# Cross-attention output projections in a two-layer encoder: seven block products inside one plan per layer

## The chip, the cores and the metric

The kernel runs on one core of one Trainium2 chip. The metric is the device time of one execution in microseconds (us), the median of the runs. Engines are named as in the profile: PE is TensorE's matrix multiply, DVE is VectorE, ACT is ScalarE, POOL is GpSimd, and SP is SyncE, whose queue issues the transfers between memory and the chip. R, X, XV, scr are buffers in SBUF; pA and pB are PSUM tiles.

## The reference, cut to what matters

The program is a two-layer encoder over 1024 tokens with 1024 channels, all in float32. Layer 0 mixes tokens by grouped-query attention, layer 1 by a pooling mixer. Both then cross-attend into 256 memory tokens and pass a gated MLP.

```
for i in range(DEPTH):                       # DEPTH = 2
    if i % N_MIXERS == 0:
        x = x + axial_gqa_attention(rmsnorm(x, attn_norm[ia]), ...)
    else:
        x = x + multiscale_pool_mixer(rmsnorm(x, pool_norm[ib]), ...)
    x = x + memory_cross_attention(rmsnorm(x, xattn_norm[i]), rmsnorm(mem, mem_norm[i]), ...)
    x = x + conv_gated_ffn(rmsnorm(x, ffn_norm[i]), ...)
return rmsnorm(x, final_norm)

def memory_cross_attention(h, mem_n, w_q, w_kv, w_o):
    q = (h @ w_q).reshape(b, s, X_HEADS, X_HEAD_DIM) * (X_HEAD_DIM ** -0.5)
    ...
    scores = jnp.einsum('bshd,bmhd->bhsm', q, k).astype(jnp.float32)
    p = jax.nn.softmax(scores, axis=-1).astype(v.dtype)
    o = jnp.einsum('bhsm,bmhd->bshd', p, v).reshape(b, s, D_MODEL)
    return o @ w_o
```

The change concerns the last line, `o @ w_o`, a product of 1024 x 1024 by 1024 x 1024 in each layer, and how the work around it is ordered.

## The kernel before

**Numbers in two halves.** PE multiplies a rounded format (fp32r), so each operand is kept as a high part, made by ACT (`high`, L667), and the rest, the low part, made by DVE as source minus high (`low`, L670). A product of two operands is three matmuls, high by high, high by low and low by high (`mm3`, L752 to L757), each of 128 rows by 512 columns. ACT comes before DVE for every operand, and both before PE.

**Slots.** High and low parts lie in 20 tiles of 2048 columns, handed out in halves (`Slots`, L88): 40 halves in all. Six scratch tiles `scr` hold what transfers bring in. Eight row tiles X0 to X7 (two of them called XV) hold the residual stream, 128 tokens each; they also serve as scratch while the stream is stored in memory (`Xq`, `Xd`).

**The plan.** `Plan` (L161) is a list scheduler that runs while the program is built. Every operation is added with its engine, a cost, what it reads and writes, the slots and PSUM banks that it takes, and perhaps a due time. PE's operations keep the order in which they are added, and PE's clock gives their due times; all others get the latest time at which their readers still come in time, and are emitted in the order in which the simulated engines could take them, at most 30 us (`AHEAD`) before they are due. The result is a fixed order for each engine and for SP's queue.

**Seven products.** `Seven` (L299) multiplies a 2 x 2 block matrix by another in seven block products instead of eight (the Strassen-Winograd form): sums S1 to S4 of the left blocks, T1 to T4 of the right ones, and results that are added up in PSUM and read between products. The query projection, the MLP's up-projection and the down-projection use it. `plan_turned` (L478) transposes a normalised row tile on PE and makes its blocks; `plan_late` (L512) makes T2 to T4; `plan_first` and `plan_early` (L580, L601) load and sum the first weights.

**The output projections.** `rows_by` (L1852) gives a block of one row tile by 512 columns: eight k-steps of `mm3`, 24 matmuls, then a DVE addition (L1864) to the row. It is called for 8 row tiles x 2 column halves. `Seven.begin` (L448) runs these 16 blocks in an order written by hand (`steps`, `turns`, `extras`, `loads`): a block, perhaps the transposes of a row tile that is done, the addition, the store of that half row (`save`, L313), and after the second half of a row the squared sum on ACT, the root on POOL and the scaling on DVE (`norm`, L317). It serves three places: layer 0's attention projection ahead of the query projection (`load_rows`, L706, loads its second column half at the start), and both layers' cross-attention projections ahead of the up-projection. Layer 1's query projection follows the pooling mixer (`pool_mixer`, L2334), which is part of a plan; it stores whole rows (L2447) before it scales them (L319).

**The cross-attention.** `cross` (L1527) plans the query products, keys and values, scores, transposes of the probabilities (`plan_turn`, L1696), and the values (`plan_values`, L1720): 16 products of 6 matmuls, whose results ACT and DVE turn into high and low parts. The weights w_o come in eight loads of 512 KB, each with one `high` and one `low` of 1024 columns (`plan_weights`). One plan ends there; the hand-written part follows; then the MLP's plan (`ffn_main`, L1899) begins. `down_sums` (L1814) loads blocks of the down-projection's weights, forms T1 to T4 on DVE and stores them in memory (`Wt`), some while the query products run; `plan_W` (L2028) loads blocks and sums back and splits them.

```
steps = ((0, 0), (0, 2), (1, 0), (1, 2), (0, 4), (1, 4), (0, 6), (1, 6),
         (0, 1), (1, 1), (0, 3), (1, 3), (0, 5), (0, 7), (1, 5), (1, 7))
turns = {3: 0, 4: 2, 6: 4, 8: 6, 10: 1, 12: 3, 15: 5}
```

Each pair is (column half, row tile); `turns` gives after which step which row tile is transposed.

Of the kernel before, what the change touches and what calls it, by code (L numbers as in the profile page):

```python
# [10 lines left out]
F32 = mybir.dt.float32  # L11
# [149 lines left out]
class Plan:  # L161
# [12 lines left out]
    def __init__(self, slots, free, room):  # L174
        self.slots = slots
        self.free = {"PE": 0.0, "DVE": 0.0, "ACT": 0.0, "POOL": 0.0, "SP": 0.0, **free}
        self.room = {pool: [0.0] * n for pool, n in room.items()}
        self.ops, self.last, self.since, self.users, self.clock = [], {}, {}, {}, 0.0
        self.known, self.pools, self.ended = {}, {}, {}

    def add(self, kind, n, emit, reads=(), writes=(), take=(), uses=(), gives=None, late=None, room=None):
# [4 lines left out]
        elif room:  # L186
# [5 lines left out]
              "begin": 0.0, "due": float("inf"), "after": [], "keys": [k for _, k in take if k] + list(uses)}  # L192
# [36 lines left out]
    def run(self):  # L229
        pools = self.pools  # L230
# [13 lines left out]
        def begin(op):  # L244
# [54 lines left out]
class Seven:  # L299
# [6 lines left out]
    def __init__(self, kn, w, columns, X, Xd, gain):  # L306
# [3 lines left out]
        self.began = False  # L310


    def save(self, n, t):  # L313
        c = slice(n * 512, (n + 1) * 512)
        self.nc.sync.dma_start(out=self.Xd[t * P:(t + 1) * P, c], in_=self.X[t][:, c])

# [4 lines left out]
    def turn(self, t):  # L321
        self.ps[t] = [self.kn.psB() for _ in range(2)]
# [4 lines left out]
    def parts(self, name, t):  # L327
        if name not in self.H:
            self.H[name] = [self.R.get(), self.R.get()]
        return (self.R.v(s, 4)[:, :, t // 2 * P:(t // 2 + 1) * P] for s in self.H[name])  # L330

    def keep(self, name, t, src):
        self.kn.hi_lo(*self.parts(name, t), src.rearrange("p (a b) -> p a b", a=4))

    def late(self, name, t):

        lo, hi = self.LO, self.HI
        src = {"T2": self.X[t][:, hi], "T3": self.X[t][:, lo], "T4": self.X[t - 1][:, hi]}[name]
        self.keep(name, t, src)
# [3 lines left out]

    def take1(self, t):
        nc, ps, lo, hi = self.nc, self.ps[t], self.LO, self.HI
        x, y = self.X[t - t % 2], self.X[t]
        nc.scalar.copy(y[:, lo], ps[0])
        if t % 2:
            self.sub(nc.vector, x[:, lo], ps[0], x[:, lo])
            self.sub(nc.vector, y[:, hi], ps[1], x[:, lo])  # L350
            self.sub(nc.vector, y[:, lo], ps[1], y[:, lo])

    def take2(self, t):
        nc, ps, lo, hi = self.nc, self.ps.pop(t), self.LO, self.HI
        x, y = self.X[t - t % 2], self.X[t]
        if t % 2 == 0:
            nc.scalar.copy(y[:, hi], ps[1])
            self.keep("B11", t, ps[0])
            self.keep("B21", t, ps[1])
        else:  # L360
            self.keep("T1", t, x[:, lo])
            self.keep("B22", t, ps[1])
            if t < 4:
                self.fourth(nc.gpsimd, t)

    def fourth(self, e, t):
        x, y, hi = self.X[t - 1], self.X[t], self.HI
        self.sub(e, x[:, hi], x[:, hi], y[:, hi])

# [6 lines left out]

    def first_load(self, f, n):

        self.raws[f] = [self.kn.scr() for _ in range(n)]
        self.place[f] = [f"raw{f}{j}" for j in range(3)]  # L380
        for j in range(min(n, 2)):
            self.load(f, j)
# [23 lines left out]
    def split(self, f, *names):  # L406
        for name in names:
            self.high(f, name)
            self.low(f, name)


# [4 lines left out]
    def product(self, f, n):  # L416
# [9 lines left out]
        bh, bl = (R.v(s, 4) for s in self.H[right])  # L426
        for k in range(4):
            self.kn.mm3(u[bank], ah[:, k], al[:, k], bh[:, k], bl[:, k], not more and k == 0, k == 3, more)
# [19 lines left out]
    def begin(self, gemm, add, free, between):  # L448

        late, split, self.began = self.late, self.split, True  # L450
        steps = ((0, 0), (0, 2), (1, 0), (1, 2), (0, 4), (1, 4), (0, 6), (1, 6),
                 (0, 1), (1, 1), (0, 3), (1, 3), (0, 5), (0, 7), (1, 5), (1, 7))
        turns = {3: 0, 4: 2, 6: 4, 8: 6, 10: 1, 12: 3, 15: 5}
        extras = {5: between,
                  13: lambda: [self.sum(0, n) for n in ("S1", "S2", "S3")],
                  14: lambda: (split(0, "A12", "A11"), late("T2", 1), late("T2", 3)),
                  15: lambda: late("T3", 1)}
        loads = {10: lambda: self.first_load(0, 3), 12: lambda: self.first_load(1, 1)}
        for i, (n, t) in enumerate(steps):
            gemm(n, t)  # L460
            free(n, t)
            u = turns.get(i)
            if u is not None:
                self.turn(u)
            extras.get(i, lambda: None)()
            add(n, t)
            self.save(n, t)
            loads.get(i, lambda: None)()
            if n:
                self.r[t] = self.kn.row_rstd(self.X[t])  # L470
            if u is not None:
                self.take1(u)
            if n:
                self.norm(t)
            if u is not None:
                self.take2(u)

    def plan_turned(self, plan, t):  # L478
# [6 lines left out]
        banks = [("turned", t, g) for g in range(2)]  # L485
# [3 lines left out]
        plan.add("turn", 8, lambda: self.turn(t), [X(t, 0), X(t, 1)], banks, [("B", k) for k in banks])  # L489
# [12 lines left out]
    def plan_keep(self, plan, name, t, src, *keys, uses=(), late=None):  # L502
        parts = lambda: self.parts(name, t)
        shaped = lambda: src().rearrange("p (a b) -> p a b", a=4)
        plan.add("copy", 512, lambda: self.kn.high(list(parts())[0], shaped()), keys, [("H", name, t)],
                 (), uses, late=late, room=None if name in self.H else (("H", name), 4))
        plan.add("add", 512, lambda: self.kn.low(*parts(), shaped()), [*keys, ("H", name, t)], [("H", name, t)], uses=uses, late=late)
# [4 lines left out]
    def plan_late(self, plan, second, third, fourth):  # L512
# [4 lines left out]
        for t in second:  # L517
            self.plan_keep(plan, "T2", t, at(self.X[t], hi), X(t, 1))
        for t in third:
            self.plan_keep(plan, "T3", t, at(self.X[t], lo), X(t, 0))  # L520
        for t in fourth:
# [5 lines left out]
    def plan_rest(self, plan):  # L527

        if self.began:
            plan.known.update({(f"X{NT - 1}", h): 5.4 for h in range(2)})  # L530
        self.plan_turned(plan, NT - 1)
        self.plan_late(plan, *((5, 7), (3, 5, 7), (5, 7)) if self.began else [(1, 3, 5, 7)] * 3)
# [1988 lines left out]
```

## Time and profile before

| | us |
|---|---|
| median of 3 runs | 2390.1 |
| lowest and highest run | 2388.69, 2391.19 |
| the profiled execution's own time | 2389.2 |
| its span, first to last instruction | 2387.5 |

The profile comes from one execution. A row of a group of instructions names its line, engine and operation, output and inputs, shapes and count, then the busy time in us and the mean of one in ns, then the engine's idle time just before and what ended it. A timeline row gives the start in us, the duration, engine, line, operation; in square brackets stands how long the engine was idle before it and for whom it waited. A window row gives, for a stretch of time, the busy time of each engine with its count of instructions. The durations of matmuls overlap, so their spacing is read from their starts.

### The profile page before, as it was taken

How to read it: one execution, taken by the hardware profiler on the slowest of the kernel's cores; microseconds unless marked ns; L12 is line 12 of the kernel's file. 1: busy time of each engine (PE TensorE's matmuls, PEld its weight loads, DVE VectorE, ACT ScalarE, POOL GpSimd, SP SyncE). 2: the span in 40 equal slices, each digit the busy share in tenths (PEclk: the TensorE clock that was granted, in tenths of full speed). 3: DMA queues.
4: the chain of work that ended last, by engine and by line, in shares of the span. 5: the costliest groups of instructions: out<-in, count | busy, mean ns of one | idle time of the engine just before them, and what ended most of it. 6: DMA issues, size and time to landing. Idle time of an engine off the chain costs nothing.

```text
span 2387.5 us, 32617 instructions
## 1 busy us (share of the span) xinstructions
PE 2373.0 (99%) x11855; PEld 1899.5 (80%) x11855; DVE 1863.1 (78%) x2608; ACT 1201.0 (50%) x1983; POOL 407.0 (17%) x393
## 2 busy tenths in 40 slices
PE   9999999999999999999999999999999999999998
PEld 8764444788988888888888888898888888888887
DVE  6679998569863898888887768986389888888875
ACT  6555556335552655455454427555255555545542
POOL 5577777210110000000000013011000000000001
PEclk9999999999999999999999999999999999999999
DMA  7000002426851243334477633695124333447852
GB/s 257 1 1 15 20 15 55 155 76 228 315 173 63 71 133 89 111 89 121 134 260 245 201 92 121 231 323 198 62 71 132 89 110 89 118 134 247 277 190 102
DMA packets 323436, 322.93 MB, mean 135 GB/s; under 512 B 32612, under 2 KB 253132, under 8 KB 323276
## 3 DMA queue, kind: packets, MB, share of 16 engines
q1 hardware_dynamic: 323132, 320.85, 41.7%
q8 instruction: 93, 1.52, 0.3%
q14 instruction: 67, 0.55, 0.1%
q10 hardware_dynamic: 144, 0.00, 0.0%
HBM read 233.30 MB, written 82.64 MB: 132 GB/s over the span
## 4 chain that ended last, share of the span: by engine, by line
PE 78%; DVE 2%; ACT 0%; DMA 0%; issue 0%; POOLq 0%; POOL 0%; DVEq 0%
PE pB L755 22%; PE pB L756 22%; PE pB L757 22%; PE pA L757 3%; PE pA L755 3%; PE pA L756 3%; PE pB L324 1%; DVE R L671 1%; PE pA L2392 0%; PE pB L1703 0%; PE pA L1703 0%; DVE X L319 0%; DMA scr<-in_ffn_w_down 0%; DVE X L342 0%; DMA Xq<-X 0%
## 5 line engine op out<-in xcount | busy, mean ns | idle before, releaser
L756 PE MATMUL pB<-R,R 128*128 128x512 f32 (+1 forms) x2735 | 1030.9, 377 | 2.6 <-DVE R L677 1.6
L755 PE MATMUL pB<-R,R 128*128 128x512 f32 (+1 forms) x2671 | 1010.6, 378 | 0.9 <-DVE R L671 0.8
L757 PE MATMUL pB<-R,R 128*128 128x512 f32 (+1 forms) x2673 | 1006.1, 376 | 0.0
L756 PEld LDWEIGHTS pB<-R,R 128*128 128x128 f32 x2735 | 515.1, 188 | 97.1 <-DVE R L677 2.6
L755 PEld LDWEIGHTS pB<-R,R 128*128 128x128 f32 x2671 | 503.0, 188 | 96.2 <-DVE R L671 1.3
L757 PEld LDWEIGHTS pB<-R,R 128*128 128x128 f32 x2673 | 503.2, 188 | 92.0 <-DVE R L671 0.5
L668 ACT ACTIVATE R<-scr 128x512 fp32r<-128x512 f32 (+3 forms) x370 | 264.5, 745 | 225.1 <-DMA scr<-Gs 55.8
L671 DVE TENSOR_TENSOR R<-scr,R 128x512 fp32r<-128x512 f32 (+2 forms) x334 | 282.1, 874 | 26.2 <-ACT R L668 22.1
L728 POOL TENSOR_SCALAR ms<-ss 128x1 f32<-128x1 f32 x52 | 12.6, 242 | 1628.8 <-ACT R L2374 629.1
L671 DVE TENSOR_TENSOR R<-X,R 128x512 fp32r<-128x512 f32 (+1 forms) x262 | 178.1, 688 | 49.3 <-ACT R L668 48.8
L668 ACT ACTIVATE R<-X 128x512 fp32r<-128x512 f32 (+1 forms) x262 | 163.8, 632 | 86.9 <-PE pB L756 53.2
L438 ACT COPY scr<-pB 128x512 f32<-128x512 f32 x156 | 91.4, 586 | 197.9 <-PE pB L757 191.2
L807 DVE TENSOR_REDUCE nm<-pS 128x1 f32<-128x512 f32 x232 | 148.2, 682 | 20.0 <-PE pS L801 18.6
L1326 ACT ACTIVATE X<-pT 128x1024 f32<-128x1024 f32 x128 | 125.1, 1023 | 72.2 <-PE pT L1319 69.6
L757 PE MATMUL pA<-R,R 128*128 128x512 f32 (+1 forms) x420 | 150.2, 358 | 0.0
L755 PE MATMUL pA<-R,R 128*128 128x512 f32 (+1 forms) x416 | 149.0, 358 | 0.0
L756 PE MATMUL pA<-R,R 128*128 128x512 f32 (+1 forms) x416 | 148.4, 357 | 0.0
L1361 PE MATMUL pO<-X,XV 128*64 128x512 f32 x512 | 124.1, 605 | 0.0
L2080 DVE TENSOR_TENSOR X<-pB,X 128x512 f32<-128x512 f32 (+1 forms) x110 | 75.2, 684 | 62.2 <-PE pB L757 61.7
L440 DVE TENSOR_TENSOR scr<-pB,scr 128x512 f32<-128x512 f32 x156 | 106.7, 684 | 11.7 <-PE pB L757 11.6
L1319 PE MATMUL pT<-R,R 64*128 64x512 f32 x768 | 103.2, 393 | 0.4 <-DVE R L671 0.4
L668 ACT ACTIVATE R<-pB 128x256 fp32r<-128x256 f32 (+1 forms) x139 | 62.6, 483 | 80.2 <-PE pB L757 43.5
(252 smaller groups left out, 2890.9 us busy)
## 6 DMA issues: line engine op xcount, KB each, us to landing
Gs<-X SPq DMA_DIRECT2D x105, 256.0 KB
X<-in_ffn_w_up SPq DMA_DIRECT2D x51, 512.0 KB
scr<-in_ffn_w_down SPq DMA_DIRECT2D x43, 512.0 KB
scr<-Gs SPq DMA_DIRECT2D x35, 512.0 KB
scr<-in_xattn_w_kv SPq DMA_DIRECT2D x32, 512.0 KB
XV<-in_ffn_w_up SPq DMA_DIRECT2D x31, 512.0 KB
scr<-Gs SPq DMA_DIRECT2D x40, 384.0 KB
Wt<-scr SPq DMA_DIRECT2D x44, 256.0 KB
```

The source lines that it names most:

```text
L438: self.nc.scalar.copy(out, p)
L440: self.nc.vector.tensor_tensor(out=out, in0=p, in1=out, op=OP.add)
L668: self.nc.scalar.activation(hi, src, AF.Copy)
L671: self.nc.vector.tensor_tensor(out=lo, in0=src, in1=hi.bitcast(F32), op=OP.subtract)
L755: mm(out, ah, bh, start=start, stop=False)
L756: mm(out, ah, bl, start=False, stop=False)
L757: mm(out, al, bh, start=False, stop=stop)
L807: nc.vector.tensor_reduce(NM[G][:, 2 * n + x.start:2 * n + x.stop], S, axis=AX.X, op=OP.max, negate=True)
L1319: nc.tensor.matmul(T[G, kt % 2][:, x * 512:(x + 1) * 512], left, right, start=first and (i, j) == (0, 0), stop=shifted or (not first and i ...
L1326: nc.scalar.activation(E[G, kt], T[G, kt % 2], AF.Exp)
L1361: nc.tensor.matmul(O[G][x * HD:(x + 1) * HD], V32[kt // 4][:, kt % 4, m // 4 * 2 + x], E[G, kt][:, x * 512:(x + 1) * 512], start=kt == 0, ...
L2080: nc.vector.tensor_tensor(out=x, in0=banks[k][:, c], in1=x, op=OP.add)
```

## The change

Both hand-written orders go (`begin`, `rows_by`, `load_rows`), and each layer becomes a single plan from its mixer's or attention's projection to the down-projection.

- **The cross-attention's projection as seven products.** The left matrix is the attention output; its blocks come straight from the value products: A11 and A12 from the even row tiles, A22 and the sums S1 to S4 as the odd ones arrive (`plan_values`). The columns of two of the four row tile pairs (group 0) are split at once; of the S sums those of group 1 are parked in memory as float32 (`Lt`) and loaded and split later (`plan_parked`, the items "L"). The right blocks and sums T1 to T4 of w_o are formed by DVE ahead of time and stored (`weight_sums`, the items "S" of ATT and the steps in OUT_AT), then loaded and split (`weight_blocks`, the items "W"). `plan_product` adds each product to its row.
- **The attention's projection** of layer 0 keeps its 16 blocks of 24 matmuls, now as planned operations in the order ATT (`attention_out`).
- **Stores.** Every row is stored in two halves as each is ready (`plan_save`), the pooling mixer's too; the squared sum goes to a slot instead of PSUM (`plan_norm`).
- **Due times.** With `follow`, the plan moves the due times of the other engines' operations by the largest delay that PE has had so far in the simulation.
- Tiles may lie in two separate halves (`get_pair`, `parts`); some transposes go to pA (`wide`); the table of the convolution is planned (`conv_table`).

```diff
+OUT = [("P", 1), ("P", 3), ("X", 0), ("G",), ("W", 0), ("V", 0, 1), ("X", 2), ("P", 5), ("V", 0, 3), ("V", 0, 0),
+       ("V", 0, 2), ("P", 7), ("V", 0, 5), ("V", 0, 7), ("V", 0, 4), ("V", 0, 6), ("X", 4), ("X", 6), ("O", 2, 0, 0),
+       ("V", 1, 0), ("V", 1, 1), ("O", 2, 0, 1), ("V", 1, 2), ("V", 1, 3), ("W", 1), ("O", 2, 1, 0), ("V", 1, 4),
+       ("V", 1, 5), ("W", 2), ("O", 2, 1, 1), ("V", 1, 6), ("O", 1, 0, 0), ("W", 3), ("X", 1), ("V", 1, 7), ("X", 3),
+       ("O", 1, 0, 1), ("O", 5, 0, 0), ("O", 5, 0, 1), ("O", 6, 0, 0), ("O", 6, 0, 1), ("O", 3, 0, 0), ("X", 5), ("X", 7),
+       ("O", 7, 0, 0), ("O", 3, 0, 1), ("O", 7, 0, 1), ("L", "S1"), ("T", 0), ("O", 4, 0, 0), ("O", 4, 0, 1), ("L", "S2"),
+       ("L", "S4"), ("L", "S3"), ("E",), ("O", 1, 1, 0), ("C",), ("O", 1, 1, 1), ("O", 5, 1, 0), ("T", 2), ("O", 5, 1, 1),
+       ("O", 6, 1, 0), ("T", 1), ("O", 6, 1, 1), ("O", 3, 1, 0), ("O", 3, 1, 1), ("T", 3), ("O", 7, 1, 0), ("O", 7, 1, 1),
+       ("T", 4), ("O", 4, 1, 0), ("T", 6), ("O", 4, 1, 1)]
+OUT_AT = (30, 42, 54, 66)
+UP = [(2, 0), 5, (1, 0), (2, 1), None]
+QUERY = [(2, 0), 5, (1, 0), (2, 1), None], [3, (2, 0), 5, (1, 0), (2, 1), None]
+ATT = [("X", 1), ("W",), ("X", 3), ("D", 0, 0), ("D", 0, 2), ("D", 0, 1), ("S",), ("D", 0, 4), ("D", 0, 3), ("D", 1, 0),
+       ("S",), ("D", 0, 6), ("D", 1, 2), ("X", 5), ("T", 0), ("S",), ("D", 1, 4), ("T", 2), ("S",), ("X", 7), ("D", 1, 6),
+       ("T", 4), ("D", 1, 1), ("D", 1, 3), ("E",), ("T", 6), ("D", 0, 5), ("T", 1), ("D", 1, 5), ("D", 0, 7), ("T", 3),
+       ("D", 1, 7)]
...
-            return t if op["engine"] == "PE" else max(t, op["due"] - self.AHEAD)
+            return t if op["engine"] == "PE" else max(t, op["due"] + drift - self.AHEAD)
...
-                    if u < t + op["busy"] and other["due"] < min(t + op["busy"], op["due"]):
+                    if u < t + op["busy"] and other["due"] < min(t + op["busy"] - drift, op["due"]):
...
+            if e == "PE" and self.follow:
+                drift = max(drift, t - op["at"])
...
+    def plan_save(self, plan, t, h):
+
+        def save():
+            c = slice(h * 512, (h + 1) * 512)
+            self.nc.sync.dma_start(out=self.Xd[t * P:(t + 1) * P, c], in_=self.X[t][:, c])
+        plan.add("load", 0.5, save, [(f"X{t}", h)], [("saved", self.tag, t, h)], late=1.0)
...
+            if not par:
+                plan_cut(plan, ("A11", "A12")[o], n, lambda: sm[b], [b], [b], 5.0)
+                plan.add("copy", 512, keep, [b], x[o:o + 1], uses=[b], late=4.0)
+                return
+            if not o:
+                plan.add("add", 512, third, [b, x[0]], s[:1], [("scr", s[0])], [b, s[0]], late=2.0)
+                return
+            plan.add("add", 512, second, [b, s[0]], s[1:], uses=[b, s[0]], late=3.0)
+            plan_cut(plan, "A22", n, lambda: sm[b], [b], [b], 5.0)
+            plan.add("add", 512, first, [s[1], x[0]], x[:1], uses=s[:1], late=5.0)
+            plan.add("add", 512, fourth, [s[1], x[1]], x[1:], uses=s[:1], late=6.0)
+            for name, t, h, k in (("S1", A, 0, x[0]), ("S2", SX, 1, s[1]), ("S4", A, 1, x[1]), ("S3", SX, 0, s[0])):
...
+                plan_cut(plan, name, n, lambda t=t, at=at: t[n][:, at:at + 256], [k], uses, 9.0 if uses else None)
+                plan.add("load", 0.25, park, [k], [("Lt", name, n)], uses=uses, late=9.0 if uses else 10.0)
...
+        def plan_product(plan, n, g, j):
+
+            left, right, bank, name, h = U.PRODUCTS[n]
+            p = 2 * g + j
+            b, t, fresh, ws = ("xo", bank, p), 2 * p + (name == "v"), n in (2, 1, 5), [("xw", k, right) for k in range(4)]
...
+                for k in range(4):
+                    self.mm3(outs[b], *(R.hv(z)[:, k * 256 + j * P:k * 256 + (j + 1) * P] for z in hs),
+                             *(R.hv(WD[k, right])[:, c] for c in (slice(0, 512), slice(512, 1024))),
+                             fresh and k == 0, k == 3, not fresh)
...
+            plan.add("product", 12, emit, ins + ws, [b], [("A" if bank == "x" else "B", b)] if fresh else (), ws + ([] if fresh else [b]),
+                     ("half", 2) if j else None)
+            plan.add("add", 512, read, [b, (f"X{t}", h)], [(f"X{t}", h)], uses=[b], late=1.5)
+            if n not in (2, 5, 6):
+                F.plan_save(plan, t, h)
+            if n in (3, 4):
+                F.plan_norm(plan, t, "fgain")
...
-            for par in range(2):
-                for m in range(NK):
-                    if not par and m % 2 == 0:
-                        plan_turn(plan, m + 1)
-                    plan_values(plan, par, m)
...
+    def attention_out(self, OT, plan, U, X):
...
+            plan.add("product", 24, gemm, [("rows", t // 4)] + [("wrow", g, k) for g in range(2) for k in range(2) if n], [b], [("B", b)],
+                     gives=("half", 8 * end + 4 * out) if end or out else None)
+            plan.add("add", 512, add, [b, *x], x, uses=[b])
+            U.plan_save(plan, t, n)
             if n:
-                free(t)
+                U.plan_norm(plan, t, "gain")
```

In OUT, "P" transposes probabilities, "V" is a value product (parity, index), "X" loads a row tile back, "W" loads and splits a group of weight blocks, "O" is a block product (product, group, tile within the group), "L" loads parked sums, "T" transposes a finished row tile, "E" starts the up-projection's first weights. In ATT, "D" is a block (column half, row tile) and "S" a round of weight sums.

More of the change, by code (lines that the diff above doesn't have):

```diff
@@ L1738, in plan_values, with keep, third @@
-            plan.add("copy", 512, lambda: self.high(list(place())[0], sm[b]), [b], [key], (), [b], late=3.0, room=(("O", par, m // 2), 2))
-            plan.add("add", 512, lambda: self.low(*place(), sm.pop(b)), [b, key], [key], uses=[b], late=3.0)
+                if last:
+                    R.put_half(*(h for z in PT.pop(par) for h in z), *(v if par else ()))
+            def keep():
+                A[n] = X[spots[n]]
+                nc.scalar.copy(A[n][:, mine], sm[b])
+            def third():
+                SX[n] = self.scr()
+                nc.vector.tensor_tensor(out=SX[n][:, :512], in0=A[n][:, :512], in1=sm[b], op=OP.subtract)
@@ L1741, in main @@
         def main():
             order, parts = U.order(nf), [(c, m) for c in range(8) for m in range(2)]
[L1743 to L1750 removed]
+            plan = Plan(R, over, {"scr": 6, "A": 2, "B": 4, "half": len(R.freed)}, True)
```

577 lines of the change are left out of this document (296 added, 281 removed).

## The prediction

> **What bounds the kernel now.** I read the page first: engine shares, busy tenths, then the chain that ended last.
>
> ```profile
> span 2387.5 us, 32617 instructions
> PE 2373.0 (99%) x11855; PEld 1899.5 (80%) x11855; DVE 1863.1 (78%) x2608; ACT 1201.0 (50%) x1983; POOL 407.0 (17%) x393
> ...
> PEclk9999999999999999999999999999999999999999
> ...
> PE 78%; DVE 2%; ACT 0%; DMA 0%; issue 0%; POOLq 0%; POOL 0%; DVEq 0%
> ```
>
> TensorE (PE) is busy 99% of the span at full clock, and the chain runs through it. So a stage is worth what its matmuls take, unless something else comes to end last there. A busy time of overlapping matmuls isn't the price of one; the timeline of a stretch without waits gives that:
>
> ```profile
> 447.42 0.39 PE L755 MATMUL pB<-R,R 128*128 128x512 f32 x1
> ...
> 452.64 0.39 PE L757 MATMUL pB<-R,R 128*128 128x512 f32 x1
> ```
>
> These are the first and last of 24 matmuls: 23 steps in 5.22 us, 0.227 us each. Next, the windows of the stages that the change touches; columns are busy time with count of PE, weight load, VectorE (DVE), ScalarE (ACT), POOL, then clock, DMA share, GB/s.
>
> ```profile
> 442.60:531.80 89.20, 87.60 (x417) 72.31 (x416) 44.60 (x57) 29.69 (x55) 10.45 (x21) 1.00 0.28 96
> 531.80:608.00 76.20, 76.20 (x363) 63.99 (x362) 72.13 (x105) 44.35 (x71) 2.44 (x4) 1.00 0.68 232
> 676.40:706.50 30.10, 30.10 (x150) 25.07 (x148) 24.88 (x36) 23.28 (x42) 1.85 (x4) 1.00 0.52 177
> 706.50:803.50 97.00, 97.00 (x462) 80.51 (x461) 45.53 (x61) 28.54 (x53) 8.54 (x18) 1.00 0.19 66
> 1190.00:1420.00 230.00, 229.90 (x1013) 189.74 (x1012) 175.36 (x243) 98.26 (x136) 2.88 (x3) 1.00 0.61 203
> 1443.00:1495.00 52.00, 49.14 (x348) 44.52 (x348) 46.62 (x69) 36.32 (x69) 12.28 (x21) 1.00 0.26 97
> ```
>
> In order: layer 0's attention projection; its query products; the cross-attention's values; its output projection; layer 0's down-projection; layer 1's pooling mixer. Only the mixer and the first leave PE idle. In the second DVE is busy 72.13 of 76.2 us (95%) and PE loses nothing: a nearly full DVE needn't cost PE anything.
>
> **The change part by part.**
>
> 1. *Fewer products.* Before, a layer's output projection is 16 blocks of 8 x 3 matmuls, 384. After: 7 products x 2 groups x 2 row tiles x 4 x 3 = 336. Two layers save 96, at 0.227 us 21.8 us. The transposes (8 per row tile, and the table's 4) and the attention projection's 384 matmuls keep their number. All of it is on the path.
>
> 2. *The attention projection inside the plan.* The waits of PE show what goes:
>
> ```profile
> 442.50 0.40 PE L755 MATMUL pB<-R,R 128*128 128x512 f32 x1
> 443.78 0.50 PE L756 MATMUL pB<-R,R 128*128 128x512 f32 x1 [0.88 <-DVE R L677]
> ...
> 445.04 0.39 PE L755 MATMUL pB<-R,R 128*128 128x512 f32 x1
> 446.15 0.50 PE L756 MATMUL pB<-R,R 128*128 128x512 f32 x1 [0.72 <-DVE R L677]
> ```
>
> The third block, the first of the right columns, waits for its weights' low parts. Its steps are 1.28 and 1.11 us instead of 0.227: 1.9 us lost. After, right columns come sixth, three blocks (16.3 us) later, while the last low part ends near 446.1: -1.9 us. What comes earlier is row tile 1's block, third instead of ninth; its input row is the first load, and only its addition needs it. New in this stage are four rounds of weight sums (2 loads of 512 KB, 4 subtractions, 4 stores of 256 KB each): 16 subtractions at 0.7 us, 11 us of DVE on 44.60 of 89.2, and 8 MB at a DMA share of 0.28. Layer 1's rounds fall into 1190 to 1420: 175 + 11 of 230 us. Hidden, 0; without that cover each late round costs PE some 0.7 us per subtraction.
>
> 3. *DVE in the new output stage.* This decides whether the 21.8 us arrive. The prices, from the groups of instructions by form (the first two and the fourth within the stages above):
>
> ```profile
> L671 DVE TENSOR_TENSOR R<-pB,R 128x512 fp32r<-128x512 f32 x20 | 13.5, 686 | 3.5 <-ACT R L668 3.5
> L671 DVE TENSOR_TENSOR R<-scr,R 128x1024 fp32r<-128x1024 f32 x7 | 8.4, 1220 | 0.5 <-ACT R L668 0.5
> L671 DVE TENSOR_TENSOR R<-scr,R 128x512 fp32r<-128x512 f32 x201 | 131.2, 685 | 11.3 <-ACT R L668 7.2 <-PE pB L757 4.1
> L1864 DVE TENSOR_TENSOR X<-pB,X 128x512 f32<-128x512 f32 x12 | 8.3, 690 | 21.2 <-PE pB L757 21.2
> L671 DVE TENSOR_TENSOR R<-pB,R 128x256 fp32r<-128x256 f32 x70 | 27.6, 418 | 25.5 <-ACT R L668 20.2 <-PE pB L801 5.2
> L1828 DVE TENSOR_TENSOR X<-X,X 128x512 f32<-128x512 f32 x20 | 13.8, 690 | 0.6
> L668 ACT ACTIVATE R<-X 128x512 fp32r<-128x512 f32 x260 | 162.2, 630 | 86.9 <-PE pB L756 53.2 <-DVE X L394 23.4 <-DMA X<-in_ffn_w_up 5.1
> L668 ACT ACTIVATE R<-pB 128x256 fp32r<-128x256 f32 x76 | 26.6, 385 | 56.4 <-PE pB L757 31.1 <-PE pB L1162 25.3
> L668 ACT ACTIVATE R<-scr 128x1024 fp32r<-128x1024 f32 x97 | 101.1, 1059 | 77.4 <-PE pB L756 32.0 <-DMA scr<-Gs 14.5 <-DMA scr<-in_xattn_w_kv 9.6
> ```
>
> Removed per layer: 16 value lows x 0.686, 8 weight lows x 1.220, 16 additions x 0.690 = 31.8 us. Added: 12 lows of A11, A12, A22 x 0.686 = 8.2; 16 sums (third, second, first, fourth) x 0.690 = 11.0; 16 half-width lows x 0.418 = 6.7; 4 parked lows x 1.220 = 4.9; 28 weight lows x 0.685 = 19.2; 28 additions x 0.690 = 19.3; together 69.3. The stage now takes 30.1 + 97.0 = 127.1 us with DVE 70.4 busy; after, PE needs 127.1 - 10.9 = 116.2 and DVE 70.4 - 31.8 + 69.3 = 107.9, or 93%. That is full, but under the 95% at which the query products lose nothing. ACT gets 28 + 12 + 8 copies of at most 0.630, 16 of 0.385 and 4 of 1.059 (40.6 us), and sheds 16 of the first and 8 of the last kind (18.6), on 23.28 + 28.54: 73.8 us, 64% of 116.
>
> The tight place: after the last value product, one output product (2.7 us) hides second sum, first sum, ACT's high and the low of S1: 0.69 + 0.69 + 0.385 + 0.418 = 2.2 us plus hand-overs. Likewise at the up-projection's start, where the last row tiles need addition, square, root and scaling. So some short waits. From both sides: 0, as in 531.8 to 608; or the mixer's rate, 2.86 of 52 us at 90% DVE, over 116 us 6.4 per layer. The query stage is the nearer row (the same seven products, planned alike), but the hand-overs are tighter: 1.5 us per layer, **+3.0**.
>
> 4. *DMA of the stage.* Removed: 8 loads of 512 KB. Added: 7 MB of weight blocks, 16 parks of 128 KB, 4 reloads of 512 KB; net 7 MB over 116 us, 60 GB/s on 66 to 177, where 232 GB/s already ran beside a full PE. SP issues some 32 more, hidden under loads planned up to 30 us ahead; the cost without that cover is the second rival below.
>
> 5. *Rows in halves; due times that move.* Layer 1's mixer has them. The chain of waits and the timeline there:
>
> ```profile
> 1444.70 4.57 DMA Xq<-X
> ...
> 1451.95 1.25 PE L324 MATMUL pB<-ident,X 128*128 128x128 f32 x8 [0.71 <-ACT XV L488]
> ```
>
> Scaling a row overwrites what the store reads, so it waits 4.57 us for a 512 KB store; two halves let the first go one block earlier and the last one be shorter. I take the 0.7 us that PE waits behind it: **-0.7**. The later waits (1463 to 1493) lie where DVE has no gap and stay. Moving due times by the delay changes only in which order ready work is taken; no row shows it. Bounds of the term: -2.9 (the mixer's whole loss goes) and +2 (an order that is worse by as much again).
>
> The Trainium skill ("DMA: Bandwidth & Descriptors", Anatomy of one DMA) gives a DMA issued from GpSimd a fixed 2.0 us plus its bytes over 436 GB/s, most of the fixed part the receipt of the write. By that a half store takes 2.6 and not half of 3.2 us, and the term would be -0.6, the sum 2368.8. The 4.57 us here is longer than its 3.2.
>
> **Sum.** The profiled execution took 2389.2 us (span 2387.5); the median of the runs shown is 2390.1, 0.9 more. 2389.2 - 21.8 - 1.9 - 0.7 + 3.0 = 2367.8, plus 0.9: **2368.7 us**.
>
> **The rivals.**
>
> *DVE ends last in the output stages.* For it: 93%, where DVE must also wait for ACT's high before each low. Against: 95% cost nothing above. At the mixer's rate, 12.8 instead of 3.0: 2378.5 us. Chance 0.17.
>
> *Slower: the one queue of SP.*
>
> ```profile
> SPq L315 <- DVE X L1864: 185.9, 35, 9.0
> ```
>
> A store at the head waits for its sum (up to 9.0 us here), and everything behind it waits too. In the new stage 16 parks and the row stores stand before the fetches of the weight groups T1/T2, B22/T3, T4, and PE's products wait for those. Six groups in two layers: if each comes more than 3.6 us late, the 21.4 us of net gain are gone; at 9.0 us each the time is 2368.7 + 54 = 2423 us. Against: loads run ahead of need, and at present the same kind of wait reaches PE nowhere. Chance 0.06. The Trainium skill ("TensorE: Matmul & The Clock Gate", Part 1) halves the clock after about 3.4 us of idleness; waits of that length would then cost more again. PE's longest waits here are near 1 us and the clock stays at 1.00, so no run shows it yet.
>
> *Cleaner than forecast.* No new wait, and the mixer's loss gone: 2368.7 - 3.0 - 2.2 = 2363.5 us. For it: the stages now planned lose almost nothing. Against: DVE is continuous in the mixer's second half. Chance 0.10.
>
> That the products don't shrink is excluded by the count.
>
> **How the numbers follow.** Forecast 0.62; rivals 0.17, 0.06, 0.10; 0.05 for a larger loss in between (0.02 still below 2385.3, 0.03 above). A measurement of this kernel can tell about 0.2%, 4.8 us, from no change. Faster 0.62 + 0.17 + 0.10 + 0.02 = 0.91, same 0.03, slower 0.06. The range goes from the cleaner case, 2363, over the DVE case to 2380: both terms at their upper bound give 2368.7 + 9.8 + 2.7 = 2381, a little past it.
>
> **What would show it.** Step 1: 96 fewer matmul records, less a few missing ones; values to eighth turn about 116 us instead of 127. Step 2: no wait for L677's successor near 443. Step 3: DVE at 90 to 95% there, PE waits under 1 us, about 1.5 in all. Step 5: the wait at 1451 gone, the later ones still there. I'm wrong if PE waits on weight loads in the output stage, or if DVE's share there is well under 90% while PE idles.

## The result and the profile after

| | before | after |
|---|---|---|
| median, us | 2390.02 | 2369.72 |
| lowest and highest run, us | 2388.69, 2391.19 | 2368.86, 2370.08 |
| the profiled execution's own time, us | 2389.2 | 2370.06 |
| its span, us | 2387.5 | 2368.3 |

The ratio is 0.9915 (95% interval 0.9898 to 0.9932): 20.3 us less, against 21.4 that the prediction's sum took off. The forecast was 2368.7.

The page of the changed kernel, its engine shares and the shares of the chain that ended last:

```profile
span 2368.3 us, 33050 instructions
PE 2352.9 (99%) x11759; PEld 1881.2 (79%) x11759; DVE 1943.0 (82%) x2798; ACT 1235.1 (52%) x2083; POOL 407.3 (17%) x387
...
PE 92%; DVE 4%; DMA 1%; ACT 1%; issue 1%; POOL 0%; SPq 0%; POOLq 0%; DVEq 0%; ACTq 0%
```

PE has 11759 matmuls for 11855, the 96 of step 1, and is still busy 99%. DVE has 80 us more, and its share of the chain went from 2% to 4%. The stages, in windows of the changed kernel (columns as before: PE, weight load, DVE, ACT, POOL, clock, DMA share, GB/s):

```profile
524.00:532.00 8.00, 8.00 (x45) 6.81 (x44) 7.44 (x12) 5.57 (x11) 2.16 (x2) 1.00 0.17 56
532.00:608.00 76.00, 75.09 (x361) 62.73 (x360) 66.92 (x95) 41.03 (x63) 3.08 (x4) 1.00 0.70 240
676.30:796.20 119.90, 118.96 (x566) 98.24 (x565) 106.53 (x174) 73.71 (x143) 10.68 (x20) 1.00 0.49 161
1190.00:1420.00 230.00, 228.53 (x1018) 188.33 (x1017) 182.71 (x258) 95.94 (x133) 5.76 (x9) 1.00 0.68 230
1622.30:1741.90 119.60, 119.08 (x565) 97.86 (x564) 106.58 (x173) 74.15 (x145) 9.77 (x20) 1.00 0.50 162
```

The third and the last row are the new output stages of the two layers, from the values to the eighth turn. The forecast was 116.2 us with DVE 107.9 busy. The new order has one more product of 2.7 us ahead of the eighth turn than the old one, so PE's share of it should be 118.9: it is 118.96, and DVE has 106.53 (89%, a little under the 90 to 95% named). The cover holds; PE is idle 0.9 us in the one and 0.5 in the other. What it waits for now, in the waits of PE (us in total, times, longest):

```profile
PE pB L696 <- DVE X L2179: 1.3, 1, 1.3
PE pB L696 <- ACT R L620: 1.1, 2, 0.7
...
PE pB L696 <- DVE XV L351: 0.8, 1, 0.8
...
PE pB L698 <- DVE R L623: 0.6, 1, 0.6
```

In the changed kernel L696 to L698 are `mm3`, L620 and L623 `high` and `low`, L2179 the addition of a down-projection's block to its row, L351 a sum of `Seven`. No wait lies near 443 any more (in the old kernel L677's successor cost 1.9 us there). Two that the forecast didn't have stand in the timeline of PE, at the start of the query products and late in layer 0's down-projection:

```profile
534.60 0.50 PE L696 MATMUL pB<-R,R 128*128 128x512 f32 x1 [0.69 <-ACT R L620]
535.33 0.50 PE L697 MATMUL pB<-R,R 128*128 128x512 f32 x1 [0.23 <-DVE R L623]
...
1260.41 0.47 PE L696 MATMUL pB<-R,R 128*128 128x512 f32 x1 [1.25 <-DVE X L2179]
```

Where the time went can be added up from the starts of matmuls. From the distance of two consecutive starts I take the spacing without waits (0.227 us for 512 columns, 0.120 for 256, 0.109 for a transpose; a missing record is one more step) and sum the steps that are more than 0.06 us over it, per stage and kernel. These are worked out from the records, one execution each. `e2`, `e6` and `e12` are experiments below: without moved due times, with whole stores in the mixer, and with both.

| stage, time in the changed kernel | before | after | e2 | e6 | e12 |
|---|---|---|---|---|---|
| attention projection, 432 to 532 | 3.1 | 0.7 | 0.7 | 0.7 | 0.7 |
| query products, 532 to 610 | 0.2 | 1.6 | 1.7 | 1.9 | 1.6 |
| output stage, layer 0, 676 to 796 | 1.6 | 3.0 | 2.4 | 2.9 | 2.4 |
| down-projection, layer 0, 1180 to 1410 | 0.7 | 2.5 | 1.8 | 0.9 | 1.8 |
| mixer, layer 1, 1433 to 1485 | 4.7 | 3.4 | 3.6 | 2.6 | 3.8 |
| output stage, layer 1, 1622 to 1742 | 2.2 | 2.7 | 3.6 | 2.3 | 4.6 |
| end of layer 1, from 2090 | 0.0 | 0.7 | 4.3 | 0.7 | 4.3 |
| whole span | 87.4 | 90.3 | 94.4 | 88.1 | 95.2 |

The whole span has 2.9 us more of such steps than before, so 21.8 - 2.9 = 18.9 us should be gained; the span is 19.2 us shorter. The row of layer 0's down-projection isn't the same from one execution to the next: the same order of instructions there lost 0.9 in `e6` and `e8` for 2.5 in the changed kernel, and 0.7 in `e10` for 2.7 in `e11`. So up to 2 us of the profiled execution is chance, not change.

### The profile page after: what moved, and what is told of

Read it like the earlier page. It is cut to its first block, busy times and chain, and to the rows that moved or that the text cites. A ratio compares the mean times of both kernels' runs of the same rounds, so it can differ in the third digit from the quotient of the medians.

```text
span 2368.3 us, 33050 instructions
## 1 busy us (share of the span) xinstructions
PE 2352.9 (99%) x11759; PEld 1881.2 (79%) x11759; DVE 1943.0 (82%) x2798; ACT 1235.1 (52%) x2083; POOL 407.3 (17%) x387
## 4 chain that ended last, share of the span: by engine, by line
PE 92%; DVE 4%; DMA 1%; ACT 1%; issue 1%; POOL 0%; SPq 0%; POOLq 0%; DVEq 0%; ACTq 0%
PE pB L696 23%; PE pB L698 23%; PE pB L697 23%; PE pO L1302 4%; PE pT L1260 4%; PE pA L696 3%; PE pA L698 3%; PE pA L697 3%; DVE R L623 2%; PE pS L742 2%; ACT R L620 1%; PE pS L1343 1%; PE pB L339 0%; DMA scr<-Gs 0%; PE pA L2489 0%
## 5 line engine op out<-in xcount | busy, mean ns | idle before, releaser
L697 PE MATMUL pB<-R,R 128*128 128x512 f32 (+1 forms) x2656 | 1000.2, 377 | 0.3 <-DVE R L623 0.2
L696 PE MATMUL pB<-R,R 128*128 128x512 f32 (+1 forms) x2594 | 981.3, 378 | 3.6 <-DVE X L2179 1.3
L698 PE MATMUL pB<-R,R 128*128 128x512 f32 (+1 forms) x2594 | 975.7, 376 | 0.6 <-DVE R L623 0.6
L697 PEld LDWEIGHTS pB<-R,R 128*128 128x128 f32 x2656 | 500.2, 188 | 92.1 <-DVE R L623 2.6
L696 PEld LDWEIGHTS pB<-R,R 128*128 128x128 f32 x2594 | 488.6, 188 | 96.6 <-ACT R L620 4.6
L698 PEld LDWEIGHTS pB<-R,R 128*128 128x128 f32 x2594 | 488.3, 188 | 90.1 <-DVE R L623 1.4
L620 ACT ACTIVATE R<-scr 128x512 fp32r<-128x512 f32 (+3 forms) x438 | 299.1, 716 | 261.3 <-DMA scr<-Gs 63.1
L623 DVE TENSOR_TENSOR R<-scr,R 128x512 fp32r<-128x512 f32 (+3 forms) x402 | 320.5, 826 | 34.1 <-ACT R L620 33.4
L669 POOL TENSOR_SCALAR ms<-ss 128x1 f32<-128x1 f32 x52 | 19.7, 379 | 1645.8 <-ACT R L2471 630.0
L623 DVE TENSOR_TENSOR R<-X,R 128x512 fp32r<-128x512 f32 (+1 forms) x299 | 192.0, 658 | 47.2 <-ACT R L620 46.8
L620 ACT ACTIVATE R<-X 128x512 fp32r<-128x512 f32 (+1 forms) x295 | 177.4, 613 | 95.9 <-PE pB L697 42.3
L696 PE MATMUL pA<-R,R 128*128 128x512 f32 (+1 forms) x452 | 162.5, 359 | 0.0
L697 PE MATMUL pA<-R,R 128*128 128x512 f32 (+1 forms) x446 | 160.1, 359 | 0.0
L698 PE MATMUL pA<-R,R 128*128 128x512 f32 (+1 forms) x444 | 159.2, 359 | 0.0
L2179 DVE TENSOR_TENSOR X<-pB,X 128x512 f32<-128x512 f32 (+1 forms) x110 | 75.1, 684 | 54.9 <-PE pB L698 54.7
L620 ACT ACTIVATE R<-pB 128x256 fp32r<-128x256 f32 (+1 forms) x144 | 66.4, 492 | 68.2 <-PE pB L698 32.4
```

The lines of the kernel that those rows point to most:

```text
L620: self.nc.scalar.activation(hi, src, AF.Copy)
L623: self.nc.vector.tensor_tensor(out=lo, in0=src, in1=hi.bitcast(F32), op=OP.subtract)
L696: mm(out, ah, bh, start=start, stop=False)
L697: mm(out, ah, bl, start=False, stop=False)
L698: mm(out, al, bh, start=False, stop=stop)
L2179: nc.vector.tensor_tensor(out=x, in0=banks[k][:, c], in1=x, op=OP.add)
```

## The experiments

All kernels are the changed one with the edit that is shown; `e11` and `e12` have two. `e1`, `e5`, `e7` and `e8` do work twice and change nothing else, to price it. Medians stand beside 2369.72 us of the changed kernel; the ratio is to the kernel before in the same series.

**e1: the eighth product given back.** One of the seven products has its twelve matmuls issued twice, 96 in all.

```diff
-                for k in range(4):
+                for k in (*range(4), *range(4)) if n == 2 else range(4):
```

> The eighth product's matmuls put back, none of its other work: in product 2 each run of 12 matmuls is issued twice (the second overwrites the first), 48 matmuls per layer, 96 in all; the plan isn't told, so every other engine keeps its order. Theory (PE bound, the saving is the 96 matmuls): +96 x 0.227 = +21.8 us less up to 2 us that the waits of the output stages shrink, so 2389.5 to 2391.5 us. Rival (the gain comes from the removed hand orders, the halved stores or the moved due times, and the stage is bound by DVE): the extra matmuls fall into DVE's time and cost under 10 us, below 2380 us.

2391.12 us (2389.99 to 2392.95), ratio 1.0006 (0.9997 to 1.0016), 11855 matmuls: 21.4 us more, for 96 x 0.227 = 21.8. The matmuls are worth their spacing, and all the rest of the change comes out near nothing: 1.5 us above the kernel before, by the interval -0.7 to 3.8.

**e5: how much room DVE has.** Every low part of the output weights (28 per layer, 0.685 us each) is made twice: 38.4 us more of DVE in the two stages.

```diff
-                self.low(*halves(WD[q, n]), raws[q, j][:, h * 512:(h + 1) * 512])
+                for _ in range(2 if tag == "xw" else 1):
+                    self.low(*halves(WD[q, n]), raws[q, j][:, h * 512:(h + 1) * 512])
```

> Each of the 28 low parts of the output projection's weights is made twice per layer (the same values), 28 x 0.685 = 19.2 us more DVE work per layer; the plan isn't told. DVE in the stage of 119.9 us goes from 106.5 to some 122 to 126 us, over what the stage holds. Theory (DVE is just under the bound there): the room left is taken and PE waits, +6 to +15 us per layer, 2382 to 2400 us. Rival (DVE has ample room, since its instructions overlap when packed): under +3 us per layer, below 2376 us.

2394.31 us (2393.6 to 2397.03), ratio 1.0019 (1.001 to 1.0028): 24.6 us more. So 38.4 - 24.6 = 13.8 us, 7 per layer, cost nothing. PE didn't wait all of the 24.6 us: the waits listed for it add up to 24.8 us, against 8.6 in the changed kernel, 16.2 more. The other 8 us go with a lower granted clock behind such waits (0.94 in the window below). By PE's waits alone the room was 22 us, 11 per layer. The two largest rows of the waits of PE:

```profile
PE pB L696 <- ACT R L620: 6.3, 4, 3.5
PE pB L697 <- DVE R L623: 5.8, 6, 2.3
```

and the window in which most of layer 0's waits lie, in `e5` and then in the changed kernel:

```profile
718.00:749.00 31.00, 24.67 (x97) 18.62 (x96) 29.98 (x51) 11.49 (x22) 1.64 (x2) 0.94 0.61 203
```

```profile
718.00:749.00 31.00, 31.00 (x145) 25.49 (x143) 23.94 (x40) 13.33 (x23) 1.49 (x4) 1.00 0.79 267
```

DVE is busy 29.98 of 31 us in `e5`, and PE only 24.67; in the changed kernel some 7 us of these 31 were free. The stage's 89% is an average: the room is set by the stretch into which the extra work falls.

**e7: the queue of SP, with a wait at its head.** Each park is stored twice to the same place, so the second store waits until the first has landed.

```diff
-                    nc.sync.dma_start(out=LT[name][:, n * 256:(n + 1) * 256], in_=t[n][:, at + 256:at + 512])
+                    for _ in range(2):
+                        nc.sync.dma_start(out=LT[name][:, n * 256:(n + 1) * 256], in_=t[n][:, at + 256:at + 512])
```

> Each of the 16 parks per layer is stored twice to the same place, so that the second store waits at the head of SP's queue for the first to land, some 2 to 4 us, and every load behind it waits too; the plan isn't told. Theory (loads run far enough ahead): under 2 us in all, 2369 to 2372 us. Rival (SP's queue stands close to ending last): 16 x 2 us of blocked queue per layer reach the weight fetches, over +10 us.

2420.12 us (2418.77 to 2422.52), ratio 1.0125 (1.011 to 1.014): 50.4 us more, slower than the old kernel. Once SP's head stands still, loads don't run far enough ahead. SP's timeline, two or four stores in a row:

```profile
715.87 4.33 SPq L1757 DMA_DIRECT2D Lt0S<-X  x4
720.31 2.12 SPq L1757 DMA_DIRECT2D Lt0S<-scr  x2
...
727.40 4.39 SPq L1757 DMA_DIRECT2D Lt0S<-XV  x4
731.84 0.43 SPq L1921 DMA_DIRECT2D scr<-in_xattn_w_o  x1
```

A pair takes 2.1 us, where the load in the last row takes 0.43; 16 pairs in a layer hold the queue for 34 us. How this reaches PE is seen in DVE's timeline and then PE's:

```profile
728.99 0.69 DVE L1729 TENSOR_TENSOR scr<-XV,pB 128x512 f32<-128x512 f32 x1 [14.93 <-DMA Lt0S<-scr]
```

```profile
729.82 0.76 PE L696 MATMUL pB<-R,R 128*128 128x512 f32 x1 [11.09 <-DVE scr L1729]
730.38 0.63 PE L697 MATMUL pB<-R,R 128*128 128x512 f32 x1
...
732.52 0.63 PE L696 MATMUL pB<-R,R 128*128 128x512 f32 x1
732.94 0.50 PE L697 MATMUL pB<-R,R 128*128 128x512 f32 x1
733.28 0.40 PE L698 MATMUL pB<-R,R 128*128 128x512 f32 x1
```

PE's longest wait is not for weights. L1729, the third sum, needs a scratch tile whose earlier contents are still to be parked, waits 14.93 us for that transfer, and the PSUM bank that it should read stays taken. The fetch of weights follows only at 731.84.

This way is taken once. The other waits of PE over 1 us in the two output stages, 2.85, 4.59, 6.97, 1.06 and 8.41 us, stand behind weights that SP fetched late, as here in SP, ACT and PE:

```profile
750.03 0.37 SPq L1921 DMA_DIRECT2D scr<-in_xattn_w_o  x1
...
753.23 1.33 ACT L620 ACTIVATE R<-scr 128x512 fp32r<-128x512 f32 x2 [8.41 <-DMA scr<-in_xattn_w_o]
```

```profile
753.91 0.79 PE L696 MATMUL pB<-R,R 128*128 128x512 f32 x1 [4.59 <-ACT R L620]
```

The list of waits of the whole kernel has both in its first rows:

```profile
PE pB L696 <- DVE scr L1729: 18.1, 2, 11.1
PE pB L696 <- ACT R L620: 18.0, 6, 8.4
```

The second wait for L1729 is the 6.97 us in layer 1, and it too begins with weights: ACT had waited 11.64 us for a transfer from `Wo`, DVE 10.81 us for ACT's high part, and the sum came right behind that low part. So PE loses 11.1 us through the scratch tile and 23.9 us through weights. Of the 50.4 us some 15 are left; most of them go with a lower granted clock behind these waits (0.93 on average from 676 to 830 us), which is shown further down.

**e8: the same bytes and issues, without the wait.** The second store goes to a place of its own, `LU`.

```diff
+        LU = {n: self.tc.dram_tile([P, D], F32, name=f"Lu{i}{n}") for n in ("S1", "S2", "S3", "S4")}
...
+                    for to in (LT, LU):
+                        nc.sync.dma_start(out=to[name][:, n * 256:(n + 1) * 256], in_=t[n][:, at + 256:at + 512])
```

> The 16 parks per layer are stored twice as in the run before, but the second store goes to a place of its own, so that no store waits for another: the same 2 MB and 16 issues more per layer without the wait at the head of SP's queue. If it was the waiting (some 2 us each) that cost 50 us: 16 x about 0.4 us of issue, hidden, within 2 us of 2369.7. If it was the number or the bytes of the stores: over 2390 us again.

SP's timeline has the two stores back to back:

```profile
705.86 0.40 SPq L1758 DMA_DIRECT2D Lt0S<-X  x1
706.30 0.45 SPq L1758 DMA_DIRECT2D Lu0S<-X  x1
```

2370.52 us (2369.88 to 2370.85), ratio 0.9916 (0.99 to 0.9933): no change: 0.8 us more, with ranges that overlap. 32 more issues and 4 MB more cost a microsecond at most; e7's 50 us are the waiting at the head.

**e2: due times that don't move.**

```diff
-            plan = Plan(R, over, {"scr": 6, "A": 2, "B": 4, "half": len(R.freed)}, True)
+            plan = Plan(R, over, {"scr": 6, "A": 2, "B": 4, "half": len(R.freed)}, False)
```

> Due times don't move with PE's delays, the rest as in the changed kernel. Theory (it changes only the order of ready work): within 3 us of 2369.7, and the 1.4 us wait near 1259, in a stretch where DVE is packed, may shrink, since without it split work is emitted earlier. Rival (the moved due times carry part of the gain): over 5 us slower, above 2375 us.

2374.24 us (2373.54 to 2375.57), ratio 0.9933 (0.9916 to 0.9949): 4.5 us more, and no run of one kernel reaches into the range of the other. Most of it lies at the end of layer 1 (0.7 to 4.3 in the table), where PE's timeline has waits that the changed kernel hasn't:

```profile
2145.10 0.50 PE L696 MATMUL pB<-R,R 128*128 128x512 f32 x1 [1.16 <-ACT scr L407]
```

```profile
2179.65 0.47 PE L696 MATMUL pB<-R,R 128*128 128x512 f32 x1 [1.57 <-DVE X L2179]
2182.68 0.50 PE L696 MATMUL pB<-R,R 128*128 128x512 f32 x1 [0.73 <-DVE XV L2179]
```

The mixer, where the prediction looked for this part, hardly differs here (3.6 and 3.4); with whole rows it does (e12).

**e3: layer 1's weight sums late.** All four rounds close together at the end of layer 0's down-projection.

```diff
-OUT_AT = (30, 42, 54, 66)
+OUT_AT = (57, 60, 63, 66)
```

> Layer 1's four rounds of weight sums come at steps 57, 60, 63 and 66 of layer 0's down-projection instead of 30, 42, 54 and 66; the same work, bunched at the end. If the sums (11 us of DVE) cause the waits of 2.5 us in that stage: the wait near 1259 goes and others come after 1340, 2368 to 2372 us. If that wait comes from the packed split work that is there anyway: it stays at about 1.4 us and the time is within 1 us of 2369.7.

2369.81 us (2367.76 to 2370.05), ratio 0.9911 (0.9896 to 0.9926): no change. The 1.25 us at 1260.41 is gone and shorter waits stand at 1198.00 (0.30 us) and 1231.42 (0.49) instead. That doesn't tell whether the sums cause it: it is gone in e6 and e8 too, where the sums stand as in the changed kernel, and none came after 1340. The sums are hidden wherever they lie.

**e4: a block of the right columns third again.** The layer-0 projection's third and sixth block change places.

```diff
-... ("D", 0, 0), ("D", 0, 2), ("D", 0, 1), ("S",), ("D", 0, 4), ("D", 0, 3), ("D", 1, 0),
+... ("D", 0, 0), ("D", 0, 2), ("D", 1, 0), ("S",), ("D", 0, 4), ("D", 0, 3), ("D", 0, 1),
```

> The first block of the right columns is third again in the attention projection, as in the kernel before (it changes places with row tile 1's block). Theory (its weights come too late for that): a wait of 1 to 3 us near 443 returns, 2370.5 to 2373 us. Rival (the plan fetches these weights early enough for any order): no wait there, 2369.7.

2374.58 us (2373.87 to 2376.51), ratio 0.9934 (0.9919 to 0.9949): 4.9 us more. The waits of step 2 come back, in the same block, but four of them, and for high parts (L620) as well as low ones (L623):

```profile
440.33 0.50 PE L696 MATMUL pB<-R,R 128*128 128x512 f32 x1 [0.24 <-ACT R L620]
442.00 0.50 PE L697 MATMUL pB<-R,R 128*128 128x512 f32 x1 [1.17 <-DVE R L623]
...
446.29 0.50 PE L696 MATMUL pB<-R,R 128*128 128x512 f32 x1 [1.43 <-ACT R L620]
447.61 0.50 PE L697 MATMUL pB<-R,R 128*128 128x512 f32 x1 [0.81 <-DVE R L623]
```

**e6: whole rows stored in the mixer.**

```diff
-                U.plan_save(plan, t, n)
+
+            def save():
+                nc.sync.dma_start(out=U.Xd[t * P:(t + 1) * P, :], in_=X[t])
+            plan.add("load", 1, save, both(t), [("saved", U.tag, t, h) for h in range(2)], late=0.0)
```

> The pooling mixer stores whole rows again, the rest as in the changed kernel. Theory (the half stores took about 0.9 us off the mixer's waits): +0.5 to +1.5 us, 2370 to 2371.5 us, with the wait back behind the first scaled row, near 1440. Rival (the mixer gained through moved due times): no change beyond 0.3 us.

2368.24 us (2366.78 to 2368.71), ratio 0.9905 (0.9891 to 0.992): 1.5 us less than the changed kernel, of which the varying down-projection of layer 0 can be a good part. The halves don't gain; in the mixer they cost. The waits of PE there with halves (the changed kernel), and then with whole rows:

```profile
1453.88 1.06 PE L339 MATMUL pB<-ident,X 128*128 128x128 f32 x8 [0.29 <-DVE X L333]
1463.24 0.39 PE L696 MATMUL pB<-R,R 128*128 128x256 f32 x1 [0.80 <-DVE XV L351]
```

```profile
1461.43 0.63 PE L339 MATMUL pB<-ident,X 128*128 128x128 f32 x4 [0.70 <-DVE XV L351]
```

**e10, e11: the query products' weights earlier.** `e10` moves the item "E" ahead of the transposes of row tile 4, against the waits at 534; `e11` is e6 and e10 together.

```diff
-       ("T", 4), ("D", 1, 1), ("D", 1, 3), ("E",), ("T", 6), ("D", 0, 5), ("T", 1), ("D", 1, 5), ("D", 0, 7), ("T", 3),
+       ("E",), ("T", 4), ("D", 1, 1), ("D", 1, 3), ("T", 6), ("D", 0, 5), ("T", 1), ("D", 1, 5), ("D", 0, 7), ("T", 3),
```

> In the attention projection the query projection's first weights are split four blocks of 5.4 us earlier. If the two waits at the start of layer 0's query products (0.85 and 0.50 us near 534) come from DVE being packed there: they shrink, 2368.0 to 2369.5 us. If they are the chain behind the last transpose itself: unchanged, 2369.7.

> Whole stores in the mixer and the earlier first weights together. If both gains are real and independent: 2367 to 2368 us, faster than the changed kernel and the one before. If the whole stores' 1.5 us was a chance of DMA times in the profile: 2369 to 2370 us.

e10: 2369.98 us (2368.67 to 2372.46), ratio 0.9916 (0.99 to 0.9933), no change; the query products still lose 1.7 us, so that place of the item is not their cause. e11: 2368.84 us (2368.07 to 2370.2), ratio 0.9908 (0.9894 to 0.9923), 0.9 less than the changed kernel, with ranges that overlap. In the records the mixer loses 2.5 us in it and 2.6 in e6, but 3.3 to 3.4 in the changed kernel, e3, e8 and e10. So with moved due times whole rows are worth 0.8 us in the mixer, twice seen; more than that is not shown.

**e12: whole rows and due times that don't move**, the edits of e6 and e2 together.

> Whole stores in the mixer and due times that don't move, the rest as in the changed kernel; its mixer is then the nearest to that of the kernel before. If the two together make up the difference between the mixers' waits (4.7 us before, 3.7 after): waits near 4.7 us between 1425 and 1485. If each acts for itself: about the 1.9 us of the whole stores alone in the mixer, and the 4.5 us of unmoved due times elsewhere, 2372 to 2374 us.

2374.99 us (2374.65 to 2376.14), ratio 0.9934 (0.992 to 0.9949): 6.8 us above e6; e2 is 4.5 above the changed kernel. The mixer loses 3.8 us, 0.9 less than before. Its waits are those of the kernel before without the first, the 0.71 us at 1451.95: 0.29, 0.73, 0.72 and 0.41 us for 0.29, 0.73, 0.71 and 0.43. The third of these is shown in the kernel before, in `e12`, and in `e2`, which has halves and unmoved due times:

```profile
1489.89 0.50 PE L756 MATMUL pB<-R,R 128*128 128x512 f32 x1 [0.71 <-DVE R L671]
```

```profile
1479.60 0.50 PE L697 MATMUL pB<-R,R 128*128 128x512 f32 x1 [0.72 <-DVE R L623]
```

```profile
1479.61 0.50 PE L697 MATMUL pB<-R,R 128*128 128x512 f32 x1 [0.17 <-DVE R L623]
```

It is gone in the changed kernel, e6 and e11, which move due times. So the first wait went with neither part, and moved due times take this one away. They are worth 1.2 us in the mixer with whole rows (3.8 and 2.6) and 0.2 with halves (3.6 and 3.4); halves cost 0.8 us with moved due times and save 0.2 without.

## Why the prediction was right, and where it was not

**Step 1, fewer products: right.** 96 fewer records, and 21.4 us when they are given back (e1), for 21.8.

**Step 2, the attention projection: right.** The wait near 443 is gone; the stage lost 2.4 us less than before, for 1.9. Its cause is the place of the right columns: with one block of them third again the waits return (e4), at 4.9 us, dearer than the old 1.9, since there ACT's high parts come late too. The weight sums are hidden, as taken (e3). What the prediction missed is the end of the stage: the first query product now waits 0.69 + 0.23 us, and the query products lose 1.4 us more than before. Why is open; e10 only excludes one place.

**Step 3, DVE in the output stage: right.** DVE 106.5 for 107.9 us; the stages lose 1.4 and 0.5 us more than before, 1.9 for the 3.0 taken. No wait of PE in them exceeds 1 us. The rival that DVE ends last was not the case, but it is nearer than its chance of 0.17 sounds: 7 to 11 us more of DVE per layer are all that fits (e5). The cleaner case, at 2363.5, was not met either: these stages lose 1.9 us more than before, and the mixer keeps 3.4 us.

**Step 4 and the slower rival: right in the outcome, wrong in the reason.** The transfers are hidden, and 4 MB more would be (e8). But "loads run ahead of need" doesn't protect: 2.1 us at the head of SP's queue per pair of stores cost 50.4 us (e7), near the 54 of the rival, which is in part luck. The rival's own way, weights that are fetched late, holds for 23.9 us of PE's waits; 11.1 us came by one that it didn't have, a scratch tile that comes free late, then DVE's third sum, then PE; and most of the other 15 us go with the clock. In the changed kernel none of PE's waits shown stands behind a park. The rival's rule of the Trainium skill can now be weighed too. After 11 us of idleness e7's matmuls start 0.43 us apart instead of 0.227, and the granted clock was 0.50 here:

```profile
731.00:733.00 2.00, 2.00 (x7) 1.52 (x6) 1.97 (x4) 0.56 (x1) 0.00 (x0) 0.50 0.22 74
```

The last matmul before the next wait, at 733.28, has again the 0.40 us of an undisturbed one, 3.5 us after the restart at 729.82. Behind that next wait, of only 2.85 us, the slow spacing is back, and again for 3.5 us:

```profile
736.52 0.78 PE L696 MATMUL pB<-R,R 128*128 128x512 f32 x1 [2.85 <-ACT R L620]
737.10 0.63 PE L697 MATMUL pB<-R,R 128*128 128x512 f32 x1
...
740.05 0.39 PE L698 MATMUL pB<-R,R 128*128 128x512 f32 x1
740.28 0.40 PE L696 MATMUL pB<-R,R 128*128 128x512 f32 x1
```

The Trainium skill ("TensorE: Matmul & The Clock Gate", Part 1) has half the clock after an idle window of about 3.4 us and the full one after as much work. The trace agrees with the way back; half the clock came after 11 us of idleness and after 2.85 us too, which is less than that window.

**Step 5: the size near, the reason wrong.** The mixer lost 1.3 us less than before, for 0.7, and the wait at 1451 is gone. But halves don't do it: that wait is gone in e12 too, with whole rows and unmoved due times. There the same whole store leaves SP at 1435.35 and its row is scaled at 1439.08, 3.7 us later, where the store before took 4.57 us to land. Why it landed sooner is not settled; the mixer now shares one plan with the query products behind it, and no run takes that away. That the term came out near its size is luck. Nor did all the later waits stay: the 0.71 us at 1489.89 went through the moved due times (e12 against e6). The chains that ended last show how long three stores took to land: a half one 2.92 us (e7, at 1484.33) and another 4.03 us (e4, at 486.32), a whole one 2.62 us (e12, at 1448.33). By the figures of the Trainium skill's "DMA: Bandwidth & Descriptors" (Anatomy of one DMA), which are for DMAs issued from GpSimd, the prediction's estimate was 2.6 us for a half store and 3.2 for a whole one; the stores here, issued by SP, scatter by more than these two differ. The term that failed most is the sentence beside it, that moving due times "changes only in which order ready work is taken": it is worth 4.5 us in all (e2), more than the 2.9 us that the term allowed for as a gain, and most of it lies outside the mixer. It is not a gain over the kernel before, though. The end of layer 1 lost nothing before, 0.7 with moved due times and 4.3 without: they keep the new, longer plan from losing there. That the cause is a due time that falls behind PE is argued from the code; the runs show the place and the size.

The sum came out 1.0 us low against the median (2368.7 for 2369.72) and 2.3 against the profiled execution (2367.8 for 2370.06), because errors partly cancelled: the query products (+1.4), the last stage (+0.7) and a varying wait in layer 0's down-projection (up to +2) against a better attention projection, mixer and output stage (-0.5, -0.6, -1.1).

## What to carry to other kernels

Where PE is busy 99%, a removed matmul is worth its spacing, but only as long as the engine that feeds it has room in the stretch where its new work falls; an experiment that doubles one of its operations says how much there is (here 7 to 11 us of 120). In a queue with one head, ask of every store whether its source is ready and what waits for it to leave, not how many bytes it has: 32 extra stores cost a microsecond at most, the same stores with a wait of 2 us each cost 50. A change in a scheduler's due times is no matter of order alone: price it by a run of its own.

## What the runs showed that I had not expected

- A park that comes late stops PE in two ways: through the buffer that it holds (a scratch tile waited for over 14.93 us cost PE 11.09 us) and through the weight fetches behind it in the queue (23.9 us of PE in five waits, e7).
- 2.85 us without work were enough for half the clock in the next 3.5 us (e7).
- With moved due times, one store of a 512 KB row in the mixer is better than two halves (0.8 us in the records), although the row's scaling must then wait for all of it. With unmoved ones it isn't (3.8 and 3.6 us).
- The same instructions in layer 0's down-projection lose between 0.7 and 2.7 us from one execution to another, more than several of the effects that were looked for.
